# A hybrid attention and SSD layer: indexer projections recorded ahead of softplus and scores, SSD state and gate in PSUM, softmax scale applied to attention's output

## The chip, the cores and the metric
The kernel runs on one core of a Trainium2 chip, in one launch. The metric is the device time in microseconds (us). In the profile PE is TensorE (matmuls) and PEld its weight loads, DVE is VectorE, ACT is ScalarE, POOL is GpSimd, and SP is SyncE, whose queue issues nearly all DMAs. Each engine works through its own instructions in order. TensorE's granted clock is 1.00 at 2.4 GHz and 0.50 at 1.2 GHz.

## The reference, cut to what matters
One decoder layer on 512 tokens of width 1024, all in float32: a normalised input goes through one large projection; a sparse attention branch and an SSD branch are gated, merged and projected; a gated MLP with a short convolution and a last norm follow. The three places of the change:
```
# indexer: 8 heads of 64; the scores choose the keys of each query
idx_logits = einsum("bqhd,bsd->bqhs", q_idx, k_idx)
score = einsum("bqhs,bqh->bqs", relu(idx_logits), w_idx)
sel = top_k(where(causal, score, -inf), 128)
# attention: 16 heads over the chosen keys of one shared latent c_kv
logits = q_lat . c_sel * scale + bias[t5_bucket(dist)]
p = softmax(logits)
att_lat = p @ c_sel ; att = att_lat @ w_uv ; y_att = att @ w_att_out
# SSD: 4 groups of 8 heads, 4 chunks of 128 tokens
dt = softplus(dt_raw + dt_bias) ; adt = dt * a ; a_cum = cumsum(adt)
h[c+1] = h[c] * exp(a_cum[c, last]) + states[c]
y = y_diag + (C @ h[c]) * exp(a_cum) + d_skip * x
u = y * silu(z) ; u = u * rsqrt(mean(u*u)) * g
```

## The kernel before, in words
Each float32 operand of a matmul is split into a rounded part and a rest: `split` (L84 to L87) rounds on ACT and subtracts on DVE or POOL. A product is then three matmuls per 128 rows of depth (`mm3`, L101: high by high, high by low, low by high). A projection of 512 tokens over 1024 inputs is 24 matmuls of 128 x 512 into one PSUM bank. `weight` (L91) loads 512 KB through SP into a ring of two buffers, rounds on ACT and subtracts on POOL into rings of three. PSUM has two rings of four banks: `mmt` for projections, `cht` ("ch") for all else.

**Head (L175 to L321).** After the first norm come projections of the indexer key and weights, of `dt` and of the latent; `pw` (L209) transposes the small ones. DVE then works out softplus by a polynomial (L240 to L255), ending in `adt`. `pac` (L258 to L260) forms cumulative sums of `adt` on PE. `latent` (L215 to L232) transposes the latent (`pcs`), takes its norm (`css` on ACT, `rsq` on DVE, `crs` on POOL), scales it (`ckv`) and transposes it back (`pckv`). `pu` makes the bias table, which is stored to DRAM (`uD`, then `skD` per head, a skewed copy). Then the loop of L303 runs over four pairs of indexer heads: weight load, projection `pqidx`, `dup_q` (L288: per head round on ACT, subtract on DVE, and copy each part to the other 64 partitions through SP, L297 and L298), and per head three score blocks `pix` on PE (L313, L314), ReLU on ACT (L316) and accumulation into `msk` on DVE (L319, L321). The top-k is a long row of max and match-replace steps on DVE, spread over the next stage.

**SSD (L342 to L625).** For each of four groups: projections `pxbc` with a convolution of four taps on DVE (L386, L388), `pz` for the gate, transposes, and for each chunk `diag` (L533: two halves of four heads into a bank `py`, two additions into `y` on DVE), `off` (L544: bank `po`, product on DVE, addition on POOL), `state` (L553: bank `pst`; the running state `Hs` in SBUF is multiplied by the chunk's decay on POOL and added to on DVE, then split) and `gate` (L570: one product of 128 x 512 in SBUF on DVE, then squares on ACT). `finish` (L597) norms and transposes; `pso` is the branch's output projection.

**Attention (L664 to L856).** Per pair of heads: keys `pk` are split into `kT` and copied by SP (L709), queries go through `dup_q`. Per head `logits` (L721) makes the bias and mask `bm` on POOL from a DMA `T`, four blocks of logits on PE (L745, L746), addition and maximum in one DVE operation (L747), exponentials with row sums on ACT (L754), and then, on DVE, reciprocals of the sums (L756) and four scalings of the probabilities (L759). `ptrans` (L764) transposes the probabilities on PE (`pPT`, L775) and splits them; `pav_` (L785) multiplies with V. There the rounded and the rest part of V give two halves of 64 partitions; one half goes through ACT and an SP copy (`atl<-ath`, L800) to the other's partitions, and `att_split` (L803) adds them (L807) and splits the result into `ath` and `atl`, on POOL for the first six pairs and on DVE for the last two. Beside it all run the gates' projections (`pgs`) and the next queries' (`pq`). After the loop `pga` and `pao` (L865) are the attention gate's and output's projections; `pao` reads all eight `ath`.

**Order.** The program records work in the order in which the code stands, with hand-made lists that weave pieces together; from it a scheduler at build time sets the order on each engine, by what depends on what and when rings of buffers come free.

Of the kernel before, what the change touches and what calls it, by code (L numbers as in the profile page):

```python
# [48 lines left out]
def _body(ctx, tc, x, prm_d, cst_d, nfin_d, wI_d, wX_d, wSO_d, wQ_d, wG_d, wAO_d, wO_d, wUp_d, wDn_d,  # L49
# [251 lines left out]

    sc = [msk[:, SEG[i]:SEG[i] + (i + 1) * P] for i in range(NB)]
    for t in range(4):  # L303
        qw = weight(wI_d[2 + t])
        ps = mmt(f"pqidx{t}")
        proj_T(ps, qw)
        qI = dup_q(ps, f"qI{t}", ("xv0", "xv1", "Ch", "Cl"), sd, 1.0, 2)
        for hh in range(2):
            h = 2 * t + hh
            for i in range(1, NB):  # L310
                n = (i + 1) * P
                pl_ = cht(f"pix{h}_{i}")[:, :n]
                nc.tensor.matmul(pl_, qI[hh][0][:, i * P:(i + 1) * P], KI[:, :n], start=True, stop=False)  # L313
                nc.tensor.matmul(pl_, qI[hh][1][:, i * P:(i + 1) * P], KI[:, :n], start=False, stop=True)  # L314
                rl = sd.tile([P, S], F32, tag="dec", name=f"rl{h}_{i}", bufs=4)
                nc.scalar.activation(rl[:, :n], pl_, AF.Relu)  # L316
                w = widx[:, i, h:h + 1]
                if h == 0:
                    nc.vector.tensor_scalar(sc[i], rl[:, :n], w, None, OP.mult)  # L319
# [155 lines left out]
    def ssd_chain(g, X, Z, uss):  # L475
# [57 lines left out]
        def diag(c, half):  # L533
            Mh, Ml = st["M"][c, half]
            X2 = st["X2"][c, half]
            py = cht(f"py{g}_{c}_{half}").rearrange("p (r t q) -> p r t q", r=4, t=2)
            for rr in range(4):
                nc.tensor.matmul(py[:, rr], Mh[:, rr, :], X2[:, rr], start=True, stop=False)
                nc.tensor.matmul(py[:, rr, 1, :], Ml[:, rr, :], X2[:, rr, 0, :], start=False, stop=True)
            yh = st["y"][c][:, 4 * half:4 * half + 4, :]  # L540
            nc.vector.tensor_tensor(yh, yh, py[:, :, 0, :], OP.add)
            nc.vector.tensor_tensor(yh, yh, py[:, :, 1, :], OP.add)

        def off(c):  # L544
            cs = slice(c * P, (c + 1) * P)
# [7 lines left out]
        def state(c):  # L553
            cs = slice(c * P, (c + 1) * P)
            BS = X["BS"]
            pst = cht(f"pst{g}_{c}")
            mm3(pst, [((BS[0][:, cs], BS[1][:, cs]), st["xw"][c])])
            p3 = pst.rearrange("p (r q) -> p r q", r=HG)
            if c == 0:
                st["Hs"] = sd.tile([P, HG, 64], F32, tag="Hs", name=f"Hs{g}", bufs=1)  # L560
                nc.vector.tensor_copy(st["Hs"], p3)
            else:
                nc.gpsimd.tensor_tensor(st["Hs"], st["Hs"], bc(cdec[:, c, hs], 64), OP.mult)
                nc.vector.tensor_tensor(st["Hs"], st["Hs"], p3, OP.add)
# [156 lines left out]
    def logits(h):  # L721
# [28 lines left out]
        def soft():  # L750
            nc.vector.tensor_scalar(mx, mx, -1.0, None, OP.mult)  # L751
            for i in range(NB):
                o, n = SEG[i], (i + 1) * P
                nc.scalar.activation(pr[:, o:o + n], pr[:, o:o + n], AF.Exp, bias=mx[:, i:i + 1],  # L754
                                     accum_out=sm[:, i:i + 1])
            nc.vector.reciprocal(sm, sm)  # L756
            for i in range(NB):
                o, n = SEG[i], (i + 1) * P
                nc.vector.tensor_scalar(pr[:, o:o + n], pr[:, o:o + n], sm[:, i:i + 1], None, OP.mult)  # L759
# [326 lines left out]
```

## Time and profile before

| what | value |
|---|---|
| median of 3 runs | 1160.88 us (1160.83 to 1161.6) |
| profiled execution | 1160.58 us, of which the span 1158.8 |
| PE busy | 1104.0 us, 95% of the span |
| DVE busy | 681.3 us, 59% |
| ACT busy | 586.0 us, 51% |
| POOL busy | 514.0 us, 44% |
| chain that ended last | PE 61%, DVE 10%, ACT 4%, issue 3%, POOL 3% of the span |

The span is the time from the first to the last recorded instruction. The head ends near 86 us, SSD near 455, attention near 657; output projections and the MLP follow. In a timeline row the last bracket is the engine's idle time ahead of the row and the instruction that released it; a row that merges several instructions says so by its count (x8). Idle time of an engine that nobody waits for costs nothing.

### The profile page before, as it was taken

What the parts mean: (1) busy time and instruction counts of PE and PEld (TensorE: products, weight loads), DVE (VectorE), ACT (ScalarE), POOL (GpSimd) and SP (SyncE); (2) the same over time, 40 slices, a digit from 0 to 9 for tenths busy, and PEclk for the clock granted to TensorE, in tenths of its full rate; (3) what the DMA queues carried; (4) which work ended last, traced back from release to release, by engine and by line L of the source; (5) the groups of instructions that cost most, each with busy time, mean ns of one, the idle gap of its engine ahead of it and who ended that gap; (6) DMA issues with size and microseconds to landing.
All of it is one profiled execution on the core that took longest, in us unless ns stands there. A gap on an engine that the chain in (4) does not pass through costs nothing.

```text
span 1158.8 us, 14580 instructions
## 1 busy us (share of the span) xinstructions
PE 1104.0 (95%) x5268; PEld 914.1 (79%) x5268; DVE 681.3 (59%) x1324; ACT 586.0 (51%) x946; POOL 514.0 (44%) x287
## 2 busy tenths in 40 slices
PE   5889998999999999999998999999999999999997
PEld 5777777788887877778887888888888888888885
DVE  5569998997589797378898623216434434430004
ACT  5355576676776665366765533226444444431123
POOL 3324243354344443557656344444444444444442
PEclk8999899999999999999999999999999999999999
DMA  5274322332333222533443233322322322322231
GB/s 188 81 195 154 109 92 73 100 94 97 118 91 97 92 94 81 164 91 107 116 126 98 58 119 127 117 91 93 107 91 92 107 93 91 108 93 91 94 107 73
DMA packets 43305, 122.06 MB, mean 105 GB/s; under 512 B 5392, under 2 KB 9760, under 8 KB 43232
## 3 DMA queue, kind: packets, MB, share of 16 engines
q1 hardware_dynamic: 42656, 120.07, 32.6%
q8 instruction: 42, 0.69, 0.3%
q10 hardware_dynamic: 576, 1.05, 0.2%
q14 instruction: 31, 0.25, 0.1%
HBM read 108.29 MB, written 5.32 MB: 98 GB/s over the span
## 4 chain that ended last, share of the span: by engine, by line
PE 61%; DVE 10%; ACT 4%; issue 3%; POOL 3%; DMA 1%; POOLq 0%; DVEq 0%; ACTq 0%
PE pup L105 21%; PE pdn L947 10%; PE pso L464 6%; PE pxbc L373 5%; PE pao L105 4%; PE pga L105 4%; PE pwo L891 3%; DVE pr L747 2%; DVE pr L759 1%; ACT pr L754 1%; PE pz L441 1%; PE pz L439 1%; PE pz L440 1%; POOL wl L87 1%; POOL bm L731 1%
## 5 line engine op out<-in xcount | busy, mean ns | idle before, releaser
L87 POOL TENSOR_TENSOR wl<-wr,wh 128x1024 fp32r<-128x1024 f32 x168 | 405.8, 2416 | 501.8 <-ACT wh L86 243.8
L86 ACT ACTIVATE wh<-wr 128x1024 fp32r<-128x1024 f32 x168 | 178.0, 1060 | 203.0 <-PE pdn L947 80.6
L930 DVE SCALAR_TENSOR_TENSOR fu<-pup,prm,fu 128x511 f32<-128x511 f32 x88 | 65.9, 749 | 124.2 <-ACT fu L928 122.6
L105 PE MATMUL pup<-hTh,wh 128*128 128x512 f32 (+1 forms) x368 | 88.0, 381 | 1.6 <-ACT hTh L144 0.9
L105 PE MATMUL pup<-hTl,wh 128*128 128x512 f32 (+1 forms) x368 | 87.7, 380 | 0.0
L105 PE MATMUL pup<-hTh,wl 128*128 128x512 f32 (+1 forms) x368 | 87.5, 380 | 0.0
L105 PEld LDWEIGHTS pup<-hTh,wh 128*128 128x128 f32 x368 | 67.2, 188 | 15.2 <-ACT hTh L144 1.1
L105 PEld LDWEIGHTS pup<-hTl,wh 128*128 128x128 f32 x368 | 67.2, 188 | 13.1
L105 PEld LDWEIGHTS pup<-hTh,wl 128*128 128x128 f32 x368 | 67.2, 188 | 13.1
L947 PE MATMUL pdn<-wl,fh 128*128 128x512 f32 x176 | 68.6, 390 | 1.2 <-POOL wl L87 1.2
L947 PE MATMUL pdn<-wh,fl 128*128 128x512 f32 x176 | 68.5, 389 | 0.0
L947 PE MATMUL pdn<-wh,fh 128*128 128x512 f32 x176 | 68.4, 390 | 0.0
L974 DVE TENSOR_TENSOR x<-pdn,x 128x512 f32<-128x512 f32 x8 | 5.5, 689 | 104.6 <-PE pdn L947 104.6
L388 DVE SCALAR_TENSOR_TENSOR u<-pxbc,prm,u 128x511 f32<-128x511 f32 (+2 forms) x72 | 53.3, 740 | 9.0 <-ACT u L386 8.7
L439 PE MATMUL pz<-wh,hTh 128*128 128x512 f32 x128 | 52.0, 406 | 3.3 <-DVE u L388 3.3
L373 PE MATMUL pxbc<-hTl,wh 128*128 128x512 f32 x192 | 51.3, 395 | 0.0
L373 PE MATMUL pxbc<-hTh,wl 128*128 128x512 f32 x192 | 51.3, 396 | 0.0
L440 PE MATMUL pz<-wl,hTh 128*128 128x512 f32 x128 | 51.0, 398 | 0.0
L441 PE MATMUL pz<-wh,hTl 128*128 128x512 f32 x128 | 50.9, 398 | 0.0
L373 PE MATMUL pxbc<-hTh,wh 128*128 128x512 f32 x192 | 50.9, 397 | 0.0
L928 ACT ACTIVATE fu<-pup,prm 128x512 f32<-128x512 f32 x44 | 34.3, 780 | 27.2 <-PE pup L105 27.2
L754 ACT ACTIVATE pr<-pr,mx 128x128 f32<-128x128 f32 (+1 forms) x64 | 35.5, 556 | 15.6 <-DVE mx L751 15.6
(359 smaller groups left out, 2547.5 us busy)
## 6 DMA issues: line engine op xcount, KB each, us to landing
wr<-wUp SPq DMA_DIRECT2D x44, 512.0 KB, 3.5
wr<-wX SPq DMA_DIRECT2D x40, 512.0 KB, 3.5
wr<-wDn SPq DMA_DIRECT2D x22, 512.0 KB, 3.4
dec<-acD SPq DMA_DIRECT2D x32, 256.0 KB, 3.4
wr<-wSO SPq DMA_DIRECT2D x16, 512.0 KB, 3.5
wr<-wG SPq DMA_DIRECT2D x16, 512.0 KB, 3.8
x<-x SPq DMA_DIRECT2D x8, 512.0 KB, 5.1
wr<-wQ SPq DMA_DIRECT2D x8, 512.0 KB, 3.5
```

The lines of the kernel that those rows point to most:

```text
L86: nc.scalar.activation(hi, src, AF.Copy)
L87: (lo_eng or nc.vector).tensor_tensor(lo, src, f(hi), OP.subtract)
L105: nc.tensor.matmul(ps, l, r, start=(i == 0), stop=(i == len(seq) - 1))
L373: nc.tensor.matmul(st["ps"], *st["it"][i], start=(i == 0), stop=(i == 23))
L388: nc.vector.scalar_tensor_tensor(u[:, d:], ps[:, :S - d], pv("cw", o + 3 - d, o + 4 - d), u[:, d:], OP.mult, OP.add)
L439: nc.tensor.matmul(ps, actT[k][0][:, bs], wh[:, ws], start=(k == 0), stop=False)
L440: nc.tensor.matmul(ps, actT[k][0][:, bs], wl[:, ws], start=False, stop=False)
L441: nc.tensor.matmul(ps, actT[k][1][:, bs], wh[:, ws], start=False, stop=(k == KD - 1))
L464: nc.tensor.matmul(ps, *seq[i], start=(i == 0), stop=(i == 11))
L754: nc.scalar.activation(pr[:, o:o + n], pr[:, o:o + n], AF.Exp, bias=mx[:, i:i + 1], accum_out=sm[:, i:i + 1])
L930: nc.vector.scalar_tensor_tensor(u[:, d:], ps[:, :S - d], pv("fw", o + 2 - d, o + 3 - d), u[:, d:], OP.mult, OP.add)
L947: nc.tensor.matmul(po8[b][hf], l[:, bs], r[:, ws], start=(k == 0 and i == 0), stop=(k == NF - 1 and i == 2))
```

## The change
It has three parts. In the head a function `pqidx` issues the next indexer projection: the first is recorded behind the copy of `crT`, the second in front of `pac`, the third and fourth behind `dup_q` of the first two. In SSD the sum of the state is made in the PSUM bank and split from there; its product with the next chunk's decay is a DVE operation out of PSUM. For chunks 1 to 3 the gate's product is made per half, out of PSUM. In attention the probabilities stay unscaled. A pair's eight columns of row sums are transposed on PE (`psm`), inverted on DVE, stored to DRAM by SP (`smD`), and broadcast back over the partitions into the `ath` tile; `att_split` multiplies by it.
```
--- before.py
+++ after.py
@@ -211,6 +211,14 @@
         nc.vector.tensor_tensor(dtS, pw[:, :, 8:40], pv("dtb").unsqueeze(1).to_broadcast([P, NB, 32]), OP.add)
         crT = n1.tile([P, S], F32, tag="crT", name="crT", bufs=1)
         nc.vector.tensor_copy(crT, psc)
+        pqs = []
+
+        def pqidx():
+            t = len(pqs)
+            pqs.append(mmt(f"pqidx{t}"))
+            proj_T(pqs[t], weight(wI_d[2 + t]))
+
+        pqidx()
 
         def latent():
             ckv = n1.tile([P, NB, 128], F32, tag="ckv", name="ckv", bufs=1)
@@ -254,6 +262,7 @@
         adt = n1.tile([P, NB, 32], F32, tag="adt", name="adt", bufs=1)
         nc.vector.scalar_tensor_tensor(adt, dtS, -1.0, av.unsqueeze(1).to_broadcast([P, NB, 32]), OP.mult, OP.mult)
         adf = adt.rearrange("p a b -> p (a b)")
+        pqidx()
         pa = cht("pac")
         nc.tensor.matmul(pa[:, 0:128], tri, adf, start=True, stop=True)
         nc.tensor.matmul(pa[:, 128:256], adf, tri, start=True, stop=True)
@@ -301,10 +310,9 @@
 
     sc = [msk[:, SEG[i]:SEG[i] + (i + 1) * P] for i in range(NB)]
     for t in range(4):
-        qw = weight(wI_d[2 + t])
-        ps = mmt(f"pqidx{t}")
-        proj_T(ps, qw)
-        qI = dup_q(ps, f"qI{t}", ("xv0", "xv1", "Ch", "Cl"), sd, 1.0, 2)
+        qI = dup_q(pqs[t], f"qI{t}", ("xv0", "xv1", "Ch", "Cl"), sd, 1.0, 2)
+        if t < 2:
+            pqidx()
         for hh in range(2):
             h = 2 * t + hh
             for i in range(1, NB):
@@ -538,8 +546,14 @@
                 nc.tensor.matmul(py[:, rr], Mh[:, rr, :], X2[:, rr], start=True, stop=False)
                 nc.tensor.matmul(py[:, rr, 1, :], Ml[:, rr, :], X2[:, rr, 0, :], start=False, stop=True)
             yh = st["y"][c][:, 4 * half:4 * half + 4, :]
-            nc.vector.tensor_tensor(yh, yh, py[:, :, 0, :], OP.add)
+            if c == 0:
+                nc.vector.tensor_tensor(yh, yh, py[:, :, 0, :], OP.add)
+                nc.vector.tensor_tensor(yh, yh, py[:, :, 1, :], OP.add)
+                return
             nc.vector.tensor_tensor(yh, yh, py[:, :, 1, :], OP.add)
+            nc.vector.tensor_tensor(py[:, :, 0, :], py[:, :, 0, :], yh, OP.add)
+            zh = Z[c][:, 256 * half:256 * half + 256].rearrange("p (r q) -> p r q", r=4)
+            nc.vector.tensor_tensor(zh, py[:, :, 0, :], zh, OP.mult)
 
         def off(c):
             cs = slice(c * P, (c + 1) * P)
@@ -556,20 +570,20 @@
             pst = cht(f"pst{g}_{c}")
             mm3(pst, [((BS[0][:, cs], BS[1][:, cs]), st["xw"][c])])
             p3 = pst.rearrange("p (r q) -> p r q", r=HG)
-            if c == 0:
-                st["Hs"] = sd.tile([P, HG, 64], F32, tag="Hs", name=f"Hs{g}", bufs=1)
-                nc.vector.tensor_copy(st["Hs"], p3)
-            else:
-                nc.gpsimd.tensor_tensor(st["Hs"], st["Hs"], bc(cdec[:, c, hs], 64), OP.mult)
-                nc.vector.tensor_tensor(st["Hs"], st["Hs"], p3, OP.add)
+            if c > 0:
+                nc.vector.tensor_tensor(p3, p3, st["Hs"], OP.add)
             Hh = sd.tile([P, S], R32, tag="Hh", name=f"Hh{g}_{c}", bufs=1)
             Hl = sd.tile([P, S], R32, tag="Hl", name=f"Hl{g}_{c}", bufs=1)
-            split(Hh, Hl, st["Hs"].rearrange("p r q -> p (r q)"), lo_eng=nc.vector)
+            split(Hh, Hl, pst)
+            if c < NB - 2:
+                st["Hs"] = sd.tile([P, HG, 64], F32, tag="Hs", name=f"Hs{g}_{c}", bufs=1)
+                nc.vector.tensor_tensor(st["Hs"], p3, bc(cdec[:, c + 1, hs], 64), OP.mult)
             st["H"] = (Hh, Hl)
 
         def gate(c):
             yf = st["y"][c].rearrange("p r q -> p (r q)")
-            nc.vector.tensor_tensor(Z[c], yf, Z[c], OP.mult)
+            if c == 0:
+                nc.vector.tensor_tensor(Z[c], yf, Z[c], OP.mult)
             nc.scalar.activation(yf, Z[c], AF.Square, accum_out=uss[:, c:c + 1])
 
         def steps(k):
@@ -670,7 +684,17 @@
             split(hi, lo, raw, lo_eng=nc.gpsimd)
             wkv.append((hi, lo))
 
-    qTs, kTs, Vs, prs, PTs = {}, {}, {}, {}, {}
+    qTs, kTs, Vs, prs, PTs, sms = {}, {}, {}, {}, {}, {}
+    smD = dram.tile([H // 2, 2 * NB, P], F32, tag="smD", name="smD")
+
+    def sums(p):
+
+        pt = cht(f"psm{p}")[:2 * NB, :P]
+        nc.tensor.transpose(pt, sms[p], ident)
+        si = ap_.tile([2 * NB, P], F32, tag="si", name=f"si{p}")
+        nc.vector.reciprocal(si, pt)
+        nc.sync.dma_start(smD[p], si)
+
     KOF = (0, 512, 1024, 896)
 
     def v_step(qd):
@@ -737,7 +761,9 @@
             nc.gpsimd.tensor_tensor(bm[:, o:o + n], msk[:, o:o + n], r31.to_broadcast([P, n]), OP.add)
         pr = ap_.tile([P, SEGW], F32, tag="pr", name=f"pr{h}")
         mx = ap_.tile([P, NB], F32, tag="mx", name=f"mx{h}")
-        sm = ap_.tile([P, NB], F32, tag="sm", name=f"sm{h}")
+        if hh == 0:
+            sms[p] = ap_.tile([P, 2 * NB], F32, tag="sm", name=f"sm{p}")
+        sm = sms[p][:, hh * NB:(hh + 1) * NB]
 
         def lg(i):
             o, n = SEG[i], (i + 1) * P
@@ -753,10 +779,6 @@
                 o, n = SEG[i], (i + 1) * P
                 nc.scalar.activation(pr[:, o:o + n], pr[:, o:o + n], AF.Exp, bias=mx[:, i:i + 1],
                                      accum_out=sm[:, i:i + 1])
-            nc.vector.reciprocal(sm, sm)
-            for i in range(NB):
-                o, n = SEG[i], (i + 1) * P
-                nc.vector.tensor_scalar(pr[:, o:o + n], pr[:, o:o + n], sm[:, i:i + 1], None, OP.mult)
             prs[h] = pr
 
         return [lambda i=i: lg(i) for i in range(NB)] + [soft]
@@ -799,12 +821,16 @@
         nc.scalar.activation(hi[o_], pav[o_], AF.Copy)
         nc.sync.dma_start(f(lo[r]), f(hi[o_]))
         nc.vector.tensor_copy(crs[p][r], pav[r])
+        if hh == 1:
+            nc.sync.dma_start(f(hi), bass.AP(tensor=smD.tensor, offset=smD.offset + p * 2 * S,
+                                             ap=[[S, 2], [0, 64], [1, S]]))
 
     def att_split(p):
         hi, lo = attT[p]
         s_ = crs[p]
         eng = nc.vector if p >= 6 else nc.gpsimd
         eng.tensor_tensor(s_, s_, f(lo), OP.add)
+        eng.tensor_tensor(s_, s_, f(hi), OP.mult)
         split(hi, lo, s_, lo_eng=eng)
 
     sds.close()
@@ -847,6 +873,8 @@
             chain.append((0, lambda: pav_(h - 2)))
         if 1 <= h <= H:
             chain += [(i == 1, s_) for i, s_ in enumerate(ptrans(h - 1))]
+            if h % 2 == 0:
+                chain.append((0, lambda: sums((h - 1) // 2)))
         if h % 4 == 1 and h < H:
             chain.append((0, v_step(h // 4)))
         chain += [(1, s_) for s_ in lg[NB:]]
```
**PE, the head.** The projections of the indexer's head pairs 0, 1 and 2 are `pqidx_439`, `_518` and `_597` before, `_359`, `_414` and `_507` now; `pac`, `pcs` and `pckv` are as above. Before:
```order
L105 MATMUL pqidx_439<-hTh_90,wl_436 128x512
L105 MATMUL pqidx_518<-hTh_76,wh_514 128x512
...
L105 MATMUL pqidx_518<-hTh_84,wh_514 128x512
L258 MATMUL pac<-adt,cs_117 128x128
L259 MATMUL pac<-cs_117,adt 128x128
L260 MATMUL pac<-adt,cs_117 128x128
L222 MATMUL pcs<-cst,crT 128x128 x4
L105 MATMUL pqidx_518<-hTh_86,wh_514 128x512
...
L105 MATMUL pqidx_518<-hTh_76,wl_515 128x512
L230 MATMUL pckv<-cst,ckv 128x128
```
Now:
```order
L105 MATMUL pqidx_359<-hTh_90,wl_363 128x512
L105 MATMUL pqidx_414<-hTh_76,wh_417 128x512
...
L105 MATMUL pqidx_414<-hTh_90,wl_418 128x512
L267 MATMUL pac<-adt,cs_117 128x128
L268 MATMUL pac<-cs_117,adt 128x128
L269 MATMUL pac<-adt,cs_117 128x128
L230 MATMUL pcs<-cst,crT 128x128 x4
L105 MATMUL pqidx_507<-hTh_76,wh_510 128x512
...
L105 MATMUL pqidx_507<-hTl_83,wh_510 128x512
L238 MATMUL pckv<-cst,ckv 128x128
```
All 24 matmuls of the second projection stand in front of `pac` now, where 5 stood; behind `pcs` come 12 of the third, where 12 of the second stood.

**SP, the head.** `wr` are weight loads, `acD` and `uD` stores of cumulative sums and of the bias table, `skD` its skewed copy, `qI0h` and `qI0l` the copies of the first pair's queries. Before:
```order
L95 DMA wr_790<-wX 128x1024
L263 DMA acD<-acT 128x128
L281 DMA uD<-us 16x383
L95 DMA wr_831<-wX 128x1024
L297 DMA qI0h_464<-qI0h_464 64x512
L298 DMA qI0l_465<-qI0l_465 64x512
L297 DMA qI0h_470<-qI0h_470 64x512
```
Now:
```order
L95 DMA wr_790<-wX 128x1024
L95 DMA wr_831<-wX 128x1024
L272 DMA acD<-acT 128x128
L290 DMA uD<-us 16x383
L636 DMA skD<-uD 128x383
L306 DMA qI0h_495<-qI0h_495 64x512
L307 DMA qI0l_496<-qI0l_496 64x512
L306 DMA qI0h_501<-qI0h_501 64x512
```
The weight load in front of `qI0h` went ahead of `acD`; one `skD`, which reads `uD`, stands in front of `qI0h`.

**SP, attention, around the keys of the sixth pair.** `qT5h` and `qT5l` are its queries, `kT` its keys, `atl` and `ath` the outputs of the fourth pair, `T` a bias tile. Before:
```order
L297 DMA qT5h_5543<-qT5h_5543 64x512
L298 DMA qT5l_5544<-qT5l_5544 64x512
L95 DMA wr_6080<-wG 128x1024
L709 DMA kT_0_5569<-kl_5568 64x512
L709 DMA kT_1_5573<-kl_5568 64x512
L800 DMA atl_4730<-ath_4729 64x512
L726 DMA T_5934<-skD 128x256
L95 DMA wr_6275<-wG 128x1024
L726 DMA T_6060<-skD 128x256
```
Now:
```order
L306 DMA qT5h_5532<-qT5h_5532 64x512
L307 DMA qT5l_5533<-qT5l_5533 64x512
L696 DMA smD<-si_5545 8x128
L733 DMA kT_0_5558<-kl_5557 64x512
L733 DMA kT_1_5562<-kl_5557 64x512
L750 DMA T_5915<-skD 128x256
L822 DMA atl_4732<-ath_4731 64x512
L825 DMA ath_4731<-smD 128x1x512
L95 DMA wr_6251<-wG 128x1024
L750 DMA T_6041<-skD 128x256
```
The store `smD` of the fourth pair's scale stands in front of the sixth pair's two `kT`, and behind the fourth pair's second `atl` comes the broadcast into its `ath`.

## Rows read from the trace of the kernel before
**Rows 1.** Stretches: from:to, length, busy (count) per engine, clock, DMA share, GB/s.
```profile
44.70:48.10 3.40, 3.40 (x13) 2.91 (x12) 1.18 (x5) 1.82 (x11) 0.00 (x0) 0.50 0.12 40
61.80:65.20 3.40, 3.40 (x12) 2.81 (x11) 1.54 (x4) 1.94 (x4) 2.38 (x1) 0.50 0.54 116
81.00:200.00 119.00, 111.08 (x513) 91.20 (x513) 113.03 (x262) 72.72 (x106) 45.70 (x22) 0.96 0.35 115
119.80:126.60 6.80, 6.80 (x24) 5.83 (x23) 6.80 (x24) 3.52 (x4) 2.37 (x1) 0.50 0.16 45
200.00:400.00 200.00, 197.96 (x989) 164.95 (x989) 164.37 (x317) 137.47 (x203) 85.05 (x42) 1.00 0.31 99
564.66:606.61 41.95, 40.69 (x220) 34.07 (x219) 36.55 (x85) 28.47 (x67) 27.61 (x26) 1.00 0.41 113
```

**Rows 2.** Timeline of PE, 33 to 119 us: start, length, line, instruction, idle before.
```profile
33.59 0.44 PE L209 MATMUL pw<-cst,sw 40*128 40x40 f32 x4
33.96 2.11 PE L105 MATMUL pqidx<-hTh,wh 128*128 128x512 f32 x8
39.55 1.29 PE L105 MATMUL pqidx<-hTh,wh 128*128 128x512 f32 x5
44.09 0.46 PE L258 MATMUL pac<-adt,cs 128*128 128x128 f32 x2 [3.24 <-issue]
...
61.08 0.76 PE L313 MATMUL pix<-KI,qI0h 128*128 128x256 f32 x3 [3.04 <-DMA qI0h<-qI0h]
...
118.79 0.47 PE L439 MATMUL pz<-wh,hTh 128*128 128x512 f32 x1 [2.39 <-DVE u L388]
```

**Rows 3.** Timeline of DVE, 42 to 87 us.
```profile
43.70 0.29 DVE L255 SCALAR_TENSOR_TENSOR adt<-dtS,av 128x128 f32<-128x128 f32 x1
...
49.20 1.13 DVE L227 SCALAR_TENSOR_TENSOR ckv<-pcs,crs,prm 128x128 f32<-128x128 f32 x4 [1.13 <-POOL crs L111]
...
81.12 5.40 DVE L321 SCALAR_TENSOR_TENSOR msk<-rl,widx,msk 128x256 f32<-128x256 f32 x6 [3.04 <-ACT rl L316]
```

**Rows 4.** Timeline of SP, the store of qI0's first half.
```profile
55.92 0.47 SPq L297 DMA_DIRECT2D qI0h<-qI0h  x1
```

**Rows 5.** Lines 541, 550, 563, 572: count: duration ns min/median/max, first and last start.
```profile
L541 DVE TENSOR_TENSOR y<-y,py x32: 400/414/422, 136.4 to 448.5; 128x256 f32<-128x256 f32 x32
L550 DVE TENSOR_TENSOR t<-po,expaq x12: 677/682/692, 152.2 to 445.2; 128x512 f32<-128x512 f32 x12
L563 POOL TENSOR_TENSOR Hs<-Hs,cdec x8: 1043/1044/1427, 141.5 to 426.3; 128x512 f32<-128x512 f32 x8
L572 DVE TENSOR_TENSOR zs<-y,zs x16: 681/822/2355, 150.0 to 449.4; 128x512 f32<-128x512 f32 x16
```

**Rows 6.** Line 759, the same columns.
```profile
L759 DVE TENSOR_SCALAR pr<-pr,sm x64: 282/414/2673, 496.6 to 648.6; 128x128 f32<-128x128 f32 x16, 128x256 f32<-128x256 f32 x16, 128x384 f32<-128x384 f32 x16, 128x512 f32<-128x512 f32 x16
```

**Rows 7.** Timeline of PE in attention, 499 to 653 us.
```profile
499.81 1.16 PE L775 MATMUL pPT<-cst,pr 128*128 128x128 f32 x6 [2.17 <-DVE pr L759]
...
587.83 0.22 PE L745 MATMUL pl<-kT,qT5h 128*128 128x128 f32 x1
...
631.20 0.44 PE L745 MATMUL pl<-kT,qT7h 128*128 128x384 f32 x1 [0.81 <-DVE V L690]
...
636.16 0.82 PE L794 MATMUL pav<-PTh,V 128*128 128x512 f32 x4 [2.73 <-DVE mx L747]
...
652.84 0.34 PE L794 MATMUL pav<-PTl,V 128*128 128x256 f32 x2
```

**Rows 8.** Timeline of SP, stores of kT and of the last ath.
```profile
581.67 2.00 SPq L709 DMA_DIRECT2D kT<-kl  x2
...
653.83 0.46 SPq L800 DMA_DIRECT2D atl<-ath  x1
```

**Rows 9.** Timeline of ACT, the last pair's rounding.
```profile
657.87 0.63 ACT L86 ACTIVATE ath<-cr 128x512 fp32r<-128x512 f32 x1 [1.49 <-DVE cr L807]
```

**Rows 10.** Tile dec, a DMA of 256 KB that repeats rows: time to landing.
```profile
DMA to landing us min/median/max: 2.9/3.4/6.3
```

More of the change, by code (lines that the diff above doesn't have):

```diff
@@ L213, in _body, with pqidx @@
         nc.vector.tensor_copy(crT, psc)
+        pqs = []
+        def pqidx():
+            t = len(pqs)
+            pqs.append(mmt(f"pqidx{t}"))
+            proj_T(pqs[t], weight(wI_d[2 + t]))
+        pqidx()
         def latent():
@@ L256, in _body @@
         adf = adt.rearrange("p a b -> p (a b)")
+        pqidx()
         pa = cht("pac")
@@ L303, in _body @@
     for t in range(4):
[L304 to L307, printed above, removed]
+        qI = dup_q(pqs[t], f"qI{t}", ("xv0", "xv1", "Ch", "Cl"), sd, 1.0, 2)
+        if t < 2:
+            pqidx()
         for hh in range(2):
@@ L540, in diag @@
             yh = st["y"][c][:, 4 * half:4 * half + 4, :]
-            nc.vector.tensor_tensor(yh, yh, py[:, :, 0, :], OP.add)
+            if c == 0:
+                nc.vector.tensor_tensor(yh, yh, py[:, :, 0, :], OP.add)
+                nc.vector.tensor_tensor(yh, yh, py[:, :, 1, :], OP.add)
+                return
             nc.vector.tensor_tensor(yh, yh, py[:, :, 1, :], OP.add)
+            nc.vector.tensor_tensor(py[:, :, 0, :], py[:, :, 0, :], yh, OP.add)
+            zh = Z[c][:, 256 * half:256 * half + 256].rearrange("p (r q) -> p r q", r=4)
+            nc.vector.tensor_tensor(zh, py[:, :, 0, :], zh, OP.mult)
         def off(c):
@@ L558, in state @@
             p3 = pst.rearrange("p (r q) -> p r q", r=HG)
[L559 to L564, printed above, removed]
+            if c > 0:
+                nc.vector.tensor_tensor(p3, p3, st["Hs"], OP.add)
             Hh = sd.tile([P, S], R32, tag="Hh", name=f"Hh{g}_{c}", bufs=1)
             Hl = sd.tile([P, S], R32, tag="Hl", name=f"Hl{g}_{c}", bufs=1)
-            split(Hh, Hl, st["Hs"].rearrange("p r q -> p (r q)"), lo_eng=nc.vector)
+            split(Hh, Hl, pst)
+            if c < NB - 2:
+                st["Hs"] = sd.tile([P, HG, 64], F32, tag="Hs", name=f"Hs{g}_{c}", bufs=1)
+                nc.vector.tensor_tensor(st["Hs"], p3, bc(cdec[:, c + 1, hs], 64), OP.mult)
             st["H"] = (Hh, Hl)
@@ L671, in load_kv, with sums @@
             wkv.append((hi, lo))
-    qTs, kTs, Vs, prs, PTs = {}, {}, {}, {}, {}
+    qTs, kTs, Vs, prs, PTs, sms = {}, {}, {}, {}, {}, {}
+    smD = dram.tile([H // 2, 2 * NB, P], F32, tag="smD", name="smD")
+    def sums(p):
+        pt = cht(f"psm{p}")[:2 * NB, :P]
+        nc.tensor.transpose(pt, sms[p], ident)
+        si = ap_.tile([2 * NB, P], F32, tag="si", name=f"si{p}")
+        nc.vector.reciprocal(si, pt)
+        nc.sync.dma_start(smD[p], si)
     KOF = (0, 512, 1024, 896)
@@ L739, in logits @@
         mx = ap_.tile([P, NB], F32, tag="mx", name=f"mx{h}")
-        sm = ap_.tile([P, NB], F32, tag="sm", name=f"sm{h}")
+        if hh == 0:
+            sms[p] = ap_.tile([P, 2 * NB], F32, tag="sm", name=f"sm{p}")
+        sm = sms[p][:, hh * NB:(hh + 1) * NB]
         def lg(i):
@@ L755, in soft @@
                                      accum_out=sm[:, i:i + 1])
[L756 to L759, printed above, removed]
             prs[h] = pr
@@ L849, in _body @@
             chain += [(i == 1, s_) for i, s_ in enumerate(ptrans(h - 1))]
+            if h % 2 == 0:
+                chain.append((0, lambda: sums((h - 1) // 2)))
         if h % 4 == 1 and h < H:
```

7 lines of the change are left out of this document (6 added, 1 removed).

## The prediction
> **What bounds the kernel now.** I read the table of stretches first: busy time of each engine and TensorE's granted clock, stretch by stretch. TensorE sets the time almost everywhere. From 200 to 400 us it is busy 197.96 of 200, and in four heads of attention 40.69 of 41.95 [rows 1]. The change takes no matmul away (it adds eight small transposes), so all it can win is TensorE's idle time, and what the clock loses after it. The reader is to look for idle time ahead of single TensorE rows, with its releaser, and for stretches in which the clock stands at 0.50. The early part has both: 3.24 us before `pac`, 3.04 before the first `pix` and 2.39 before a `pz` [rows 2]; and behind each of the three the clock is at 0.50, for 3.4, 3.4 and 6.8 us [rows 1]. At 1.2 GHz a stretch that is busy throughout does half its work, so it loses half its length: 1.7, 1.7 and 3.4 us. Between 81 and 200 us VectorE is as full as TensorE (113.03 against 111.08 of 119); from 200 us on it has slack [rows 1]. Then I read the two chains behind the head's waits, and the waits in attention.
>
> **Part 1, projections ahead of softplus and scores (term: 10.9 us gained).** The wait before `pac` is for `adt`, the end of VectorE's softplus chain, at 43.70 + 0.29 = 43.99 [rows 3]. TensorE had only 24 + 5 projection matmuls to put in front of it. 24 of them take 39.55 − 33.96 = 5.59 us [rows 2], so 0.233 each; 19 more are put in front now, 4.4 us, and cover the 3.24 us wholly. The price is that `pac` begins about 4.4 − 3.24 = 1.2 us later, and the latent chain behind it with it. Before, its normalised latent was ready at 49.20 + 1.13 = 50.33 [rows 3]; now at about 51.5. TensorE reaches `pac` at 33.96 + 48 × 0.233 = 45.1, has ten small passes for `pac` and `pcs` there (2.3 us by the 0.46 of the first two; less where the clock is full) and 12 projection matmuls (2.8 us) in front of `pckv`: 50.2. So a new wait of 1.3 us, or up to 2.5, appears there; I take 1.2, the slip alone.
>
> The first `pix` waits for a DMA of `qI0h` that was issued at 55.92 and released TensorE at 61.08, 5.16 us later [rows 2, 4]. On SP a weight load stands right in front of that issue; it goes out earlier now, and one `skD` stands there in its place, which waits for the store `uD` ahead of it; both engines that make `qI0` are busy meanwhile, so I charge it to the 0.5 us below. Before the first `pix` TensorE has 15 matmuls more, 3.5 us, against 3.04 us of idle. Since the latent chain, which the rounding of `qI0` follows on ScalarE and VectorE, is itself later, I leave 0.5 us of this wait: 2.54 gained. With both waits gone their half-clock stretches go: 2 × 1.7 = 3.4. The scores' accumulations on VectorE, which ended at 81.12 + 5.40 = 86.5 [rows 3], then end some 8 us earlier, and the conv that the `pz` at 118.79 waits for (2.39 us, and 3.4 of clock, 5.8 together) comes sooner. VectorE is 95% busy between, so I take half: 2.9. Sum: 3.24 + 2.54 + 3.4 + 2.9 − 1.2 = 10.9. Its bounds: 4 (the `pac` wait and one clock stretch, less the new wait) to 15.
>
> **Part 2, SSD (term: 1 us gained).** Per group, VectorE loses one copy of a state and gains two products of the state with its decay out of PSUM: 4 × 0.68 off, 8 × 0.68 on, by the price of a 128x512 operation on PSUM [rows 5]: 2.7 us more. GpSimd loses 8 products of 1.04, 8.3 us, and each stood between two operations of VectorE. The gate of chunks 1 to 3 becomes 24 products of 256 columns out of PSUM for 12 of 512 out of SBUF: 24 × 0.414 = 9.9 for 12 × 0.822 = 9.9, nothing. All of this lies beside matmuls; TensorE idles 2.04 us in 200 us there [rows 1]. I take half of that. The other side: a state's PSUM bank is held through the split and the product, about 2.0 us longer (ScalarE 0.63, two of VectorE 0.68 each). Twelve such holds, each felt with 0.28 us, would cost 3.4: bounds −3 to +5, the upper one from idle in the stretch from 81 to 200 us (7.92 us in all) that is not yet counted.
>
> The row of the gate product shows 681 ns at least, 822 in the median and 2355 at most; an operation of 256 columns from PSUM never goes over 422 [rows 5]. The Trainium skill (VectorE: DVE Perf Modes, "The TRN2 errata") speaks against cutting it: the cost per instruction is fixed, and many small tiles pay it for each. By that rule, against the undisturbed 681, the gate would cost 12 × (0.83 − 0.68) = 1.8 us more of VectorE and this term would be about nothing; by the median row it stays at 1. I go by the median.
>
> **Part 3, attention (term: 4.6 us gained).** 64 scalings and 16 reciprocals leave VectorE; the scalings alone take 414 ns in the median and up to 2673 [rows 6]. TensorE waits for them directly once, 2.17 us; 0.81 and 2.73 us stand behind a late VectorE while it does two scalings beside GpSimd [rows 7]. I count all three: 5.71. In the steady four heads 1.26 us idle remain [rows 1]; two such fours, half gained: 1.2. Added on TensorE: 8 transposes of the sums to 8 rows; four transposes of 40 columns take 0.44 us [rows 2], so 8 × 0.11 = 0.9. Per pair, a reciprocal of 8x128 on VectorE, one multiply of 128x512 (GpSimd's for six pairs, VectorE's for two) and one 8-row store on SP are hidden: the four heads leave VectorE 5.4 and GpSimd 14.3 us free [rows 1]. The store waits for the reciprocal, and a later pair's `kT` loads stand behind it on SP: they went out at 581.67 and ended by 583.67, and the first `pl` on them comes at 587.83 [rows 7, 8], 4.2 us later, less a landing of 2 to 3; a store of 0.5 us fits. The broadcast waits on SP for the second `atl` and only weight loads and a bias tile stand behind it.
>
> The last pair is not covered. Its last `pav` ends at 652.84 + 0.34 = 653.18, the store of `ath` goes out at 653.83, and ScalarE gets the sum at 657.87 [rows 7 to 9], so `atl` is there about 0.7 + 0.1 earlier, 657.1. Only then the broadcast of the scale may overwrite `ath`. A broadcast of this size took 2.9 to 6.3 us to land, 3.4 in the median [rows 10]: 660.3. A multiply (0.68) and a rounding (0.63) more: 661.7, with hand-overs 662.0, so 8.8 after the `pav`. The program puts 32 matmuls there before those that read it, 32 × 0.233 = 7.4: 1.4 us of waiting, from 0.5 up to 4. Sum: 5.71 + 1.2 − 0.9 − 1.4 = 4.6. Bounds: 0 to 7.
>
> **Sum.** The profiled execution takes 1160.58 us, its span 1158.8 and 1.8 around it; the median of the runs is 1160.88, 0.3 higher. 10.9 + 1 + 4.6 = 16.5, so 1160.58 − 16.5 = 1144.1. I forecast 1144.
>
> **Rivals.**
> - *VectorE gives the head start back.* TensorE is early at 81 us, but until 200 us VectorE must do 113 us of work in 119; TensorE then waits for convs and splits instead. Then of part 1 only VectorE's own idle is won, the 3.04 us before its last accumulations [rows 3], and one clock stretch of 1.7: 4.7 in place of 10.9, 1150. For it: the 95%. Against: the projections and scores that come earlier are what VectorE idles for.
> - *More goes.* The `pz` wait goes with all its clock (2.9 more), and the idle between 81 and 200 us shrinks by 3 more: 1138. For it: the accumulations end 8 us earlier and GpSimd's link leaves the state chain. Against: the same full VectorE.
> - *It does not do what it says.* The waits only move, from `pac` to `pckv`, from `pix` to the next DMA, from the scalings to the exponentials: within 2 us of before, 1160. For it: five matmuls were already in front of `pac`, so the order was filling gaps. Against: 19 more matmuls are there to be seen.
> - *PSUM banks turn it slower.* States and both halves of the gate now keep their banks until VectorE has finished with them; if each of the 12 holds reaches TensorE with its 2.0 us, 24 us are lost and, with 15.5 won by parts 1 and 3, the time is about 1169. It turns slower from 15.5 / 12 = 1.3 us of wait per hold. For it: VectorE is 82% busy there and works in order. Against: TensorE waits for next to nothing between 200 and 400 us, and three other banks are in the ring. The Trainium skill (TensorE: Matmul & The Clock Gate, "A second HAM failure mode: psum-queue depth-cycling") adds that many short idles on a bank ring can also drop the clock; this trace has 1.00 over those 200 us [rows 1], so nothing of it shows before the change.
>
> **How the numbers follow.** Forecast 0.50 (its own range 1140 to 1148), VectorE gives back 0.18, more goes 0.14, waits only move 0.08, banks 0.10. The range from 1136 to 1155 holds the first three. A measurement of this kernel tells some 0.2%, 2.3 us, from no change: faster 0.82, same 0.08, slower 0.10.
>
> **What would show it.** Right: no idle over 1 us before `pac` or the first `pix`, no clock of 0.50 near 45 and 62 us, the last accumulations by 79 us, at most 41.5 us for four heads, a wait of 1 to 2 us before the matmuls that read the last `ath`, and no wait for `kT`. Wrong: a new wait before `pckv` with the clock at 0.50 behind it; TensorE idle between 85 and 200 us grown by what the head won; `pst`, `py` or `po` waiting for a release by VectorE; a wait behind the scale's broadcast ahead of the last pair.

## The result and the profile after

The changed kernel takes 1186.66 us in the median (1185.72 to 1188.72, 4 runs); the kernel before 1160.86. The ratio is 1.0234, 95% interval [1.0215, 1.0252]: 27 us slower by the ratio (25.8 by the medians), where 16 us faster was forecast. The profiled execution has a span of 1187.0.

The time is in one stage. The first logits (`pl`) start at 472.4 us instead of 486.1, so head and SSD won 13.7 us. From there to the last `pav` attention takes 202.7 us instead of 167.1, 35.6 more, and from there to the end of the last `pao` (768.55, just behind the last stretch shown) 93.5 instead of 87.2, 6.2 more. The table of stretches, after: an SSD stretch, attention, and the stretch behind it (columns as in [rows 1]):
```profile
200.00:400.00 200.00, 198.42 (x990) 165.42 (x989) 162.03 (x333) 143.33 (x208) 81.95 (x38) 1.00 0.31 104
472.40:675.10 202.70, 166.75 (x857) 141.59 (x858) 114.11 (x262) 106.67 (x256) 109.49 (x94) 0.91 0.34 97
675.10:768.30 93.20, 89.55 (x378) 72.33 (x378) 27.83 (x25) 27.11 (x33) 35.90 (x15) 0.97 0.32 106
```
The same two stretches, before:
```profile
486.10:653.20 167.10, 158.25 (x850) 132.00 (x851) 141.03 (x333) 108.73 (x256) 102.46 (x88) 1.00 0.37 104
653.20:740.40 87.20, 87.20 (x378) 70.48 (x378) 28.96 (x24) 27.12 (x33) 36.29 (x15) 1.00 0.34 117
```
In attention TensorE's idle time is 202.7 − 166.75 = 35.9 us, against 8.85 before. The other 8.5 us are in its busy time, which grew with only the eight `psm` added as work: the mean clock fell to 0.91. VectorE is *less* busy (114 against 141 us): the engines wait for one another.

The head answers to [rows 2] so, on PE after:
```profile
45.60 0.38 PE L267 MATMUL pac<-adt,cs 128*128 128x128 f32 x2
...
51.10 0.33 PE L238 MATMUL pckv<-cst,ckv 128*128 128x128 f32 x1 [1.51 <-DVE ckv L235]
...
60.00 0.70 PE L321 MATMUL pix<-KI,qI0h 128*128 128x256 f32 x3
...
111.81 0.47 PE L447 MATMUL pz<-wh,hTh 128*128 128x512 f32 x1 [1.13 <-DVE u L396]
```
and by stretches:
```profile
44.00:52.00 8.00, 6.49 (x33) 4.73 (x31) 3.71 (x11) 2.99 (x12) 3.40 (x2) 1.00 0.43 134
51.00:56.00 5.00, 4.90 (x15) 3.47 (x16) 2.06 (x6) 1.80 (x3) 0.00 (x0) 0.66 0.13 42
60.00:64.00 4.00, 4.00 (x21) 3.37 (x21) 1.92 (x5) 3.21 (x8) 0.00 (x0) 1.00 0.90 210
111.00:118.00 7.00, 6.20 (x35) 5.41 (x36) 7.00 (x25) 3.56 (x4) 2.40 (x1) 1.00 0.14 53
```
The waits before `pac` and before the first `pix` are gone; the new wait before `pckv` is there, 1.51 us, and behind it the clock is at 1.2 GHz for a part (0.66 in the mean of 51 to 56). The `pz` wait is 1.13 instead of 2.39, and the clock stays at 1.00.

Now the loss. The chain that ended last, one pair of heads of it (start, length, what):
```profile
587.75 2.40 DMA atl<-ath
...
590.16 8.18 DMA ath<-smD
...
598.47 1.30 POOL cr L833
...
599.79 0.04 ACT ath L86
599.84 0.50 issue
600.33 1.04 ACT wh L86
601.37 0.88 ACT pr L780 x4
...
602.27 0.60 ACT ath L821
...
602.97 0.68 DVE cr L823
```
The reader is to see one transfer of 8.18 us in it, `ath<-smD`, behind the landing of `atl`; behind it follow one engine after another. GpSimd and ScalarE at the same place, after:
```profile
598.47 1.29 POOL L833 TENSOR_TENSOR cr<-cr,ath 128x512 f32<-128x512 f32 x1 [4.55 <-DMA ath<-smD]
```
```profile
599.79 0.63 ACT L86 ACTIVATE ath<-cr 128x512 fp32r<-128x512 f32 x1 [8.01 <-POOL cr L833]
```
GpSimd idles 4.55 us ahead of its multiply. ScalarE idles 8.01 us ahead of its rounding of the product (L86); behind that stand, in its queue, the exponentials of a later head and the copy of `pav`, behind these VectorE's copy of `pav` into `cr` (L823), and TensorE stands before `psm` for a release by that copy. `psm` reads nothing that the copy writes; what the copy sets free is, by the code, the PSUM bank of `pav` in the ring `ch`.

A second thing holds that copy back. `cr` has one buffer (L820), so the next pair's first copy into it has to wait until GpSimd's subtraction, the last to read the old sum, is done. Here that is at 600.50 + 1.28 = 601.78, only 1.2 us before the copy starts at 602.97, and for one pair the profile names the subtraction as the releaser; after:
```profile
600.50 1.28 POOL L87 TENSOR_TENSOR atl<-cr,ath 128x512 fp32r<-128x512 f32 x1 [0.74 <-ACT ath L86]
```
```profile
651.08 0.68 DVE L823 COPY cr<-pav 64x512 f32<-64x512 f32 x1 [3.84 <-POOL atl L87]
```
Both the queue and the buffer wait for the same transfer; no run separates what each would cost alone.

Six of the eight `psm` wait for that copy. The last pair's waits for VectorE's `PTl`, which stands on VectorE behind a multiply (L833) that waits for the broadcast. PE, after, four of the seven, the last pair's among them, and the last wait, before `pao`:
```profile
523.06 0.38 PE L693 MATMUL psm<-cst,sm 128*8 128x128 f32 x1 [5.80 <-DVE cr L823]
...
577.42 0.38 PE L693 MATMUL psm<-cst,sm 128*8 128x128 f32 x1 [6.92 <-DVE cr L823]
...
603.70 0.27 PE L693 MATMUL psm<-cst,sm 128*8 128x128 f32 x1 [3.95 <-DVE cr L823]
...
671.60 0.37 PE L693 MATMUL psm<-cst,sm 128*8 128x128 f32 x1 [5.39 <-DVE PTl L801]
...
686.96 0.79 PE L105 MATMUL pao<-ath,wh 128*128 128x512 f32 x1 [3.65 <-ACT ath L86]
```
The seven sum to 34.7 us, the `pao` wait is 3.65.

### The profile page after: what moved, and what is told of

The parts are those of the page before. It is cut to its first block, busy times and chain, and to the rows that moved or that the text cites. A ratio compares the mean times of both kernels' runs of the same rounds, so it can differ in the third digit from the quotient of the medians.

```text
span 1187.0 us, 14556 instructions
## 1 busy us (share of the span) xinstructions
PE 1109.8 (94%) x5276; PEld 922.1 (78%) x5276; DVE 645.8 (54%) x1270; ACT 587.2 (49%) x948; POOL 511.4 (43%) x285
## 4 chain that ended last, share of the span: by engine, by line
PE 42%; DMA 4%; POOL 2%; ACT 1%; DVE 1%; issue 0%; POOLq 0%; DVEq 0%; SPq 0%; ACTq 0%
PE pup L105 20%; PE pdn L975 10%; PE pao L105 4%; PE pwo L919 3%; DMA ath<-smD 3%; PE pga L105 3%; DMA atl<-ath 1%; PE pgs L381 1%; POOL wl L87 1%; POOL cr L833 0%; POOL bm L755 0%; ACT pr L780 0%; ACT wh L86 0%; ACT ath L821 0%; PE pl L771 0%
## 5 line engine op out<-in xcount | busy, mean ns | idle before, releaser
L86 ACT ACTIVATE wh<-wr 128x1024 fp32r<-128x1024 f32 x168 | 177.9, 1059 | 210.7 <-PE pdn L975 80.6
```

Source lines behind the costliest of these rows:

```text
L86: nc.scalar.activation(hi, src, AF.Copy)
```

## The experiments

The theory (A): the transfer of the scale is long, and through GpSimd's multiply and ScalarE's rounding, each of which stands in a queue that is worked through in order, it holds back the next heads. Rivals: (B) part 2's longer hold of PSUM banks costs; (C) the added multiply, transposes and stores cost by themselves.

**e1: parts 1 and 2, attention as before.** Edit: part 3 taken back.
```
-        nc.sync.dma_start(smD[p], si)
+            nc.vector.reciprocal(sm, sm)
+                nc.vector.tensor_scalar(pr[:, o:o + n], pr[:, o:o + n], sm[:, i:i + 1], None, OP.mult)
-        eng.tensor_tensor(s_, s_, f(hi), OP.mult)
...
```


> Parts 1 and 2 alone, attention as before. Theory A (the whole loss is in attention, where the broadcast of the scale holds GpSimd and ScalarE): the first logits come at 472 instead of 486 us as in the changed kernel, attention then takes the 167 us it took before, so about 1160.9 - 14 = 1147 us. Theory B (PSUM banks held longer by part 2 also cost, later): 1160 us or more.


Measured: 1144.51 us, ratio 0.9861 [0.9842, 0.9879], 16 us faster. Attention in its profile is as before, 167.1 us and 8.7 idle:
```profile
470.90:638.00 167.10, 158.36 (x850) 132.05 (x851) 141.04 (x333) 108.91 (x256) 102.48 (x88) 1.00 0.37 104
```
The loss is part 3's alone; B falls.

**e2: part 3 alone.** Edit: part 3 put into the kernel before, so of the changed kernel
```
-        pqidx()
-        pqidx()
+                nc.gpsimd.tensor_tensor(st["Hs"], st["Hs"], bc(cdec[:, c, hs], 64), OP.mult)
+            nc.vector.tensor_tensor(Z[c], yf, Z[c], OP.mult)
...
```


> Part 3 alone, head and SSD as before. Theory A: attention takes the 203 us and the tail the 6 us more of the changed kernel, so 1160.9 + 42 = 1203 us. Theory B: part 3 is nearly free by itself, about 1160 us.


Measured: 1207.04 us, ratio 1.0403 [1.0380, 1.0427]: 46 us slower, a little more than expected. In its profile attention takes 206.9 us and the stretch to the end of the last `pao` 95.0, against 202.7 and 93.5 in the changed kernel. So the loss comes without parts 1 and 2 as well.

**e3: no transfer.**
```
-        if hh == 1:
-            nc.sync.dma_start(f(hi), bass.AP(tensor=smD.tensor, ...
-        eng.tensor_tensor(s_, s_, f(hi), OP.mult)
+        eng.tensor_tensor(s_, s_, f(actT[0][0]), OP.mult)
```


> All three parts, but the broadcast of the scale is left out and the multiply reads a tile that is there already (the attention output is not scaled by the sums). All other instructions of part 3 stay. Theory A (the wait for the transfer): the waits of 4 to 7 us ahead of each psm go, 1140 to 1147 us. Theory C (the added multiply on GpSimd, the transposes and the store cost by themselves): still over 1170 us.


Measured: 1148.16 us, ratio 0.9897 [0.9875, 0.9920]. That is 1 us above the range expected from theory A. With every other instruction of part 3 in place 38.5 us of the changed kernel's time go with the transfer, so C falls as the cause. Attention has 8.75 us of idle, as much as before the change:
```profile
471.10:640.20 169.10, 160.35 (x857) 135.08 (x857) 116.02 (x262) 107.59 (x256) 110.61 (x94) 0.98 0.38 106
```
and it lies elsewhere; PE, e3:
```profile
619.93 0.63 PE L797 MATMUL pPT<-cst,pr 128*128 128x128 f32 x2 [3.74 <-DVE mx L773]
...
636.97 0.28 PE L693 MATMUL psm<-cst,sm 128*8 128x128 f32 x1 [2.29 <-DVE cr L823]
```
So part 3 shows no win even with a free transfer (e1 and its repeat e9, without part 3, take 1144.5 and 1147.6): where TensorE waited for scalings it now waits for VectorE's maximum and for `cr`.

**e4: two transfers of 64 partitions.**
```
-            nc.sync.dma_start(f(hi), bass.AP(..., offset=smD.offset + p * 2 * S, ap=[[S, 2], [0, 64], [1, S]]))
+            for k in range(2):
+                nc.sync.dma_start(f(hi[64 * k:64 * k + 64]), bass.AP(..., offset=smD.offset + (2 * p + k) * S,
+                                                                     ap=[[0, 64], [1, S]]))
```


> The broadcast as two transfers of 64 partitions, one per head, each from one row. If the 7.4 to 8.2 us of the transfer come from the form with two source rows in one descriptor list, the landing falls to the 3.4 us of the decay's broadcast and the time to about 1186.7 - 7 x 4 - 4 = 1155 us. If they come from the source or the queue, the landing stays at 7 us or more and the time within 4 us of 1186.7.


Measured: 1154.14 us, ratio 0.9939 [0.9919, 0.9959], as expected from the form. The broadcast among e4's DMA issues (count, KB each, median us to landing):
```profile
ath<-smD SPq DMA_DIRECT2D x16, 128.0 KB, 2.9
```
where the changed kernel's chain has 7.4 to 8.2. Attention falls to 174.7 us:
```profile
473.10:647.80 174.70, 161.59 (x857) 135.54 (x858) 117.23 (x263) 107.06 (x257) 110.96 (x94) 0.98 0.40 113
```

**e7: one transfer from one row.**
```
-ap=[[S, 2], [0, 64], [1, S]]
+ap=[[0, P], [1, S]]
```


> The broadcast as one transfer of 256 KB again, but from one row for all 128 partitions, the form of the decay's transfer (the second head of a pair gets the first head's scale). If the two-row form is what made the transfer slow, it lands in 2.9 to 3.8 us and the time is that of the two transfers, 1154 us, within 3. If it is the single transfer of 256 KB or its source, the landing stays over 7 us and the time near 1187.


Measured: 1151.97 us (2 runs, ratio 0.9926 [0.9900, 0.9952]). The same row of e7:
```profile
ath<-smD SPq DMA_DIRECT2D x8, 256.0 KB, 3.1
```
The same 256 KB to the same tile are there in 3.1 us, so neither size nor source is slow but the form with two rows. In stretches in which SP issued nothing else beside that transfer the profile shows the difference (last three columns: clock, DMA share, GB/s). After:
```profile
510.40:514.00 3.60, 3.60 (x20) 3.07 (x19) 2.40 (x6) 0.04 (x1) 3.57 (x2) 1.00 0.11 39
590.80:593.90 3.10, 3.10 (x16) 2.60 (x16) 2.69 (x4) 0.98 (x2) 3.10 (x2) 1.00 0.09 36
```
e7, the same kind of stretch:
```profile
506.40:509.10 2.70, 2.70 (x14) 2.29 (x13) 2.07 (x5) 0.32 (x1) 2.70 (x2) 1.00 0.40 97
528.90:531.60 2.70, 2.70 (x15) 2.32 (x14) 1.95 (x4) 0.23 (x1) 2.70 (x2) 1.00 0.34 97
```
A share of 0.09 to 0.11 of sixteen DMA engines is less than two engines, at 36 to 39 GB/s; in the one-row form the share is 0.34 to 0.40 and the rate 97. The Trainium skill (DMA: Bandwidth & Descriptors, "Rules for kernel authors") says that an outermost dimension of few elements, as a leading broadcast of c copies, confines a DMA to at most c engines. The source here has an outermost dimension of 2, and the trace agrees. The same section advises against two transfers to disjoint halves of the partitions, on the ground that both halves use all sixteen engines anyway. The two-row form did not use them all, so here the halves brought 7.4 us down to 2.9; against one transfer from one row they win nothing (1154.1 and 1152.0 us).

**e5 and e6: part 1 alone, part 2 alone.** Edits to the kernel before, e5 and then e6:
```
+        pqidx()
...
+            nc.vector.tensor_tensor(zh, py[:, :, 0, :], zh, OP.mult)
+                nc.vector.tensor_tensor(st["Hs"], p3, bc(cdec[:, c + 1, hs], 64), OP.mult)
...
```


> Part 1 alone. The first pz came 5.8 us earlier in the changed kernel and the first py 8.8 us earlier, with a first norm that ended 0.7 us later. If the head keeps all of it, 1160.6 - 10 = 1150.6 us, and part 2 is worth the remaining 6 of the 16 us. If VectorE gives the head start back without part 2, at most 5 us are won: 1156 us or more.

> Part 2 alone. If the two parts add up, the 16.1 us of both less those of part 1: 1160.6 - 6 = 1154.6 us. By the term of 1 us that was forecast for it: 1159.6 us. If held PSUM banks cost by themselves: over 1161 us.


Measured: part 1 alone 1157.86 us, ratio 0.9980 [0.9969, 0.9990], 2.3 us by the ratio; part 2 alone 1156.55 us, ratio 0.9956 [0.9938, 0.9973], 5.1 us by the ratio (2.0 and 3.3 by the medians). They do not add up: 7.4 for both apart, 16.1 in e1 (12.2 in e9, the same kernel again). In e5 the first `pst` comes 8.1 us earlier than before (129.0 against 137.1), `pyT` 5.6 and the first `pl` 2.5. The stretch from 137 to 205 us of before, e5 and e1, in this order:
```profile
137.00:205.00 68.00, 63.67 (x313) 52.31 (x312) 63.84 (x140) 50.67 (x73) 27.69 (x15) 0.97 0.26 87
```
```profile
137.00:205.00 68.00, 60.80 (x302) 49.11 (x301) 63.92 (x134) 48.58 (x71) 26.46 (x14) 1.00 0.24 83
```
```profile
137.00:205.00 68.00, 64.89 (x332) 53.78 (x331) 66.97 (x150) 51.05 (x76) 26.46 (x13) 1.00 0.28 94
```
VectorE is busy 63.8 to 67.0 of the 68 us in all three, however early TensorE arrives; in e5 TensorE gets 60.80 us in, before 63.67, in e1 64.89. The gate's product out of SBUF, before and in e5 (same columns as the page's part 5), and the `pz` wait of e5:
```profile
L572 DVE TENSOR_TENSOR zs<-y,zs 128x512 f32<-128x512 f32 x4 | 4.3, 1075 | 0.0
```
```profile
L580 DVE TENSOR_TENSOR zs<-y,zs 128x512 f32<-128x512 f32 x4 | 6.3, 1577 | 0.0
```
```profile
193.59 0.47 PE L447 MATMUL pz<-wh,hTh 128*128 128x512 f32 x1 [2.90 <-DVE u L396]
```

**e10 and e11: part 1 with one half of part 2.** Edits to e1, e10 and then e11:
```
-            nc.vector.tensor_tensor(zh, py[:, :, 0, :], zh, OP.mult)
+            nc.vector.tensor_tensor(Z[c], yf, Z[c], OP.mult)
...
-                nc.vector.tensor_tensor(st["Hs"], p3, bc(cdec[:, c + 1, hs], 64), OP.mult)
+                nc.gpsimd.tensor_tensor(st["Hs"], st["Hs"], bc(cdec[:, c, hs], 64), OP.mult)
...
```


> Part 1 with the state half of part 2 (sum in PSUM, decay product on VectorE, GpSimd's product gone), gate as before. Part 1 alone won 2 us, parts 1 and 2 13 to 16. If the state chain through GpSimd is what gave the head start back, most comes with this half: 1147 to 1150 us. If the gate's product out of SBUF, stretched to 2.4 us beside GpSimd, gave it back: 1155 us or more.

> Part 1 with the gate half of part 2 (products of 256 columns out of PSUM for chunks 1 to 3), state as before. By the first theory 1155 us or more; by the second 1147 to 1150 us. If both halves are needed, each of the two runs stays over 1152 us.


Measured: with the state half 1148.69 us, ratio 0.9906 [0.9882, 0.9930]; with the gate half 1146.54, ratio 0.9874 [0.9858, 0.9891]. Neither theory holds alone, and both halves are not needed together: each lets most of the head start through, 11 and 15 us. Why one of them is enough stays open. From 137 to 205 us the gate's products take 6.3 us of VectorE in e5, 3.7 with the state half (4 of 0.92) and 4.7 with the gate half (one of 2.25, six of 0.41); TensorE gets 63.2 and 64.0 us in. Whether this shorter work on VectorE is what does it is not shown: VectorE is busy 63.5 and 66.3 us there, against 63.9 in e5.

**e8 and e9: one scaling on ScalarE, and e1 again.**
```
+                if i == 3:
+                    nc.scalar.activation(pr[:, o:o + n], pr[:, o:o + n], AF.Copy, scale=sm[:, i:i + 1])
+                else:
                     nc.vector.tensor_scalar(pr[:, o:o + n], pr[:, o:o + n], sm[:, i:i + 1], None, OP.mult)
```


> Parts 1 and 2, attention as before, but the largest of a head's four scalings (128x512) runs on ScalarE instead of VectorE. In parts 1 and 2 alone TensorE still waits 2.16, 0.80 and 2.71 us behind scalings and some 0.9 us in each steady four heads. If VectorE's time is what it waits for, most of these 7 us go: 1138 to 1142 us. If ScalarE, which must do the exponentials and the roundings of the transposed probabilities, becomes the late one: 1144.5 us or more.

> Parts 1 and 2 alone once more, beside the variant with one scaling on ScalarE: 1144.5 us, within 2.


Measured: e8 1143.83 us, ratio 0.9864 [0.9847, 0.9881]; e9 1147.62, ratio 0.9894 [0.9875, 0.9913]. Both are faster than the kernel before; between the two the intervals overlap, and e8 lies between its two expectations. e9 missed its own by 3 us, though it is e1's kernel. In the profiles attention takes 162.7 us in e8, and 169.6 in e9 where e1 had 167.1:
```profile
469.70:632.40 162.70, 156.81 (x849) 131.73 (x849) 133.97 (x318) 118.78 (x273) 99.56 (x88) 1.00 0.38 106
```
```profile
469.80:639.40 169.60, 160.92 (x850) 134.66 (x851) 142.65 (x333) 108.79 (x257) 102.55 (x88) 0.98 0.37 102
```
TensorE's idle time there is 8.7 us in e9 as in e1; only the clock differs, 0.98 and 1.00. So differences of 3 us between variants are not read as an effect here. In e8 a part is given back at the last pair, PE, e8:
```profile
640.62 0.50 PE L105 MATMUL pao<-ath,wh 128*128 128x512 f32 x1 [2.23 <-ACT ath L86]
```

## Why the prediction was wrong

- **The step that failed is in part 3**: the broadcast of the scale was put at nothing for seven of the eight pairs. The prediction says that "one multiply of 128x512 (GpSimd's for six pairs, VectorE's for two) and one 8-row store on SP are hidden". The busy shares left room for the multiply itself, and e3 shows that it fits. What it waits for was not asked, nor who stands behind it: I named what is queued behind the broadcast on SP, but not GpSimd's multiply and ScalarE's rounding, which wait for its landing in order, with exponentials and the copy of `pav` behind, nor the one buffer of `cr`. The runs showed 34.7 us of waits ahead of `psm` in its place. The 4.6 us that attention was to win became a loss of 41.8 by the stretches (35.6 and 6.2); with the 13.7 won ahead of it that is the 28 us by which the span grew. The prediction's last sign of being wrong, a wait behind the scale's broadcast, came in full size, but no rival and no price stood for it.
- **The landing was mis-sized too.** From the decay's broadcast [rows 10] I took 3.4 us for the last pair, bounds 2.9 to 6.3; it was 7.4 to 8.2. That row is a transfer from one row. This is the larger part: with the landing as I had taken it (e7, 3.1) the time is 1152, 35 us less, and inside the range. Even then the waits ahead of `psm` sum to 12.3 us, so "hidden" fails at the forecast landing too. e3, with no transfer, has 3.7 us of them; its time is 4 us below e7, but the intervals overlap. What the slow form would cost if nobody stood behind the multiply was not tried.
- **The tail**: the wait before the last `ath` was forecast at 1.4 (0.5 to 4) and is 3.65, behind a landing of 7.43. The other 2.6 us that this stretch lost are busy time at a mean clock of 0.97, for which nothing was charged. In the sum of the forecast 657.1 + 3.4 is 660.5, not 660.3; it changes 1.4 to 1.6.
- **The scalings**: 5.71 + 1.2 us of waits were to go. They went, and others of the same sum came (e3). Freeing VectorE was not worth what its waits showed.
- **Parts 1 and 2**: 11.9 us forecast, 13.7 in the changed kernel by the first `pl`, 16.1 and 12.2 measured alone. The sum held, its split did not, so that it held is in part luck. Alone, part 1 is worth 2.3 and not 10.9: the rival that VectorE gives the head start back is what happens without part 2, whose term of 1 is worth 10 to 14 beside it. Within part 1, the `pac` term was right, the `pix` wait went wholly in this run (1.96 are left in e1), the new wait (1.2 forecast, 1.51) had a fall of the clock behind it that I had not charged (in e1 the same wait had none), and the accumulations ended at 83.4 instead of 79 us.
- **The rivals**: the slower one put the cause in PSUM banks of SSD. That the time came out on its side is luck, for its mechanism was not the cause: the stretch from 200 to 400 us kept 198.4 of 200 busy, and e1 has the longer holds and is faster. Its sign did come, small: before 250 us one `py` waits 1.33 us for VectorE's product of a state, and one `po` 1.02 us for an addition into `y`; PE, after:
```profile
154.63 0.47 PE L546 MATMUL py<-X,Mh 128*128 128x128 f32 x1 [1.33 <-DVE Hs L580]
...
233.16 0.47 PE L105 MATMUL po<-Hh,Ch 128*128 128x512 f32 x1 [1.02 <-DVE y L551]
```
  PSUM banks did matter in attention, where `psm` waits for that of `pav`. The store of the sums in front of `kT` cost nothing, as forecast: no wait for `kT` appears.

## What to carry to other kernels

Busy shares say whether an added instruction fits, not when it can start: for each operand that a new instruction waits for, follow the queues of the engine that waits and of those that wait for it, and the buffers that it holds meanwhile. A broadcast is priced by a row of the same form, outermost dimension included, not of the same size. Two edits on the same full engine may be worth little apart and much together, so a part's term should be worked out with the other parts in place.

## What the runs showed of the hardware

- A DMA of 256 KB whose source has an outermost dimension of 2 took 7.4 to 8.2 us at a share of some 0.10 of the DMA engines; as two transfers 2.9, from one row 3.1.
- A reciprocal on VectorE of 8x128 took 0.94 us, nearly as long as the 0.95 of one of 128x128 in the kernel before; one of 128x4 took 0.18. Leaving out rows saved nothing there, leaving out columns did.
- Behind the wait of 1.51 us before `pckv` the granted clock was 0.66 in the mean of five us, a part of them at 1.2 GHz; behind the same wait of 1.51 us in e1 it stayed at 1.00 (50 to 55 us), as behind the 1.13 us before `pz`. So the length of that wait alone did not decide it. The wait and the stretch of e1:
```profile
49.78 0.33 PE L238 MATMUL pckv<-cst,ckv 128*128 128x128 f32 x1 [1.51 <-DVE ckv L235]
```
```profile
50.00:55.00 5.00, 5.00 (x23) 3.69 (x23) 1.76 (x5) 2.32 (x4) 0.80 (x1) 1.00 0.08 24
```
